# The second MLP product with seven block products in place of eight, every one of them summed over all pairs in PSUM

## The chip, the core and the metric

The kernel runs on one core of one Trainium2 chip (trn2). The metric is the time of one execution in device microseconds; it is given as the median of three runs. One further execution was profiled.

## The reference

One decoder block in float32 on a sequence of 1024 tokens with 1024 channels: three token mixers with gates, and then the MLP, the only part that the change touches:

```python
h = rmsnorm(x, g_mlp[l])
hid = jnp.square(jax.nn.relu(jnp.einsum("bsd,df->bsf", h, w_mlp_in[l])))
x = x + jnp.einsum("bsf,fd->bsd", hid, w_mlp_out[l])
...
return rmsnorm(x, g_final)
```

`w_mlp_in` (W1) is 1024 x 4096 and `w_mlp_out` (W2) is 4096 x 1024.

## The kernel before

Every float32 matrix is cut into two parts in a rounded format: ACT copies the value into `hi` (L96), and another engine takes the difference, `lo` = value - `hi` (L110 and L979). A product is then three matmuls, hi x hi, hi x lo and lo x hi (`mm3`, L151 to L153). A matmul here has 128 x 128 stationary and 128 x 512 moving elements. A tile scheduler orders every engine's instructions at build time, by priorities (`band`; band "w" goes first) and by its own model; on the chip each engine runs its list strictly in that order. SP's list is the queue of all DMAs: an issue whose buffer isn't free yet holds up every later one.

**First product** (`up_pair`, L1094 and on). The 4096 hidden columns are 16 pairs of 128-column blocks, the 1024 tokens two halves. A pair's four results, c11, c12 (first column block, token halves 1 and 2) and c21, c22, come from seven block products of 12 matmuls each instead of eight; for the first ten pairs (`EARLY`) the two that need no sums were made before, so that five are left. `load_pair` loads four 512 KB or 256 KB pieces of W1 (r0 to r3), POOL makes the four sums (L1086 to L1089), ACT and DVE cut them into hi and lo. The results sit in `hid{c}` (buffers `braw`, two). DVE clamps and squares them (L1125, L1127), and SP stores the pair to `hid_d` in DRAM, one DMA per pair.

**Second product** (`mlp_down`, L1165 and on). Eight chunks of four 128-row blocks of W2. `load_down` loads a chunk's hidden values (two loads of 1024 KB, `hr`, into `braw`) and W2 rows (four of 512 KB, `wr`); ACT makes `hhi` and `whi`, DVE `hlo`, POOL `wlo` (all 128 x 1024). For each of 8 token tiles and 2 column halves, 12 matmuls go into a PSUM bank, which DVE adds to the residual `x2` (L1181): 8 x 8 x 2 x 12 = 1536 matmuls of 512 columns (the last token tile's second half is cut in two). In the last chunk each finished token tile is normed at once: squares on ACT (L1184), a Newton root of ten small DVE operations (`rsqrt_newton`, L127 and on), the scaling of half 0 on DVE (L972) and of half 1 on ACT (L974) and POOL (L975), and the store.

The kernel has one pool, `E`, for the second product's operands; it takes the memory of the first product's (`h2T`, T2 to T4), so its first tiles wait for the first product's last matmuls.

## Time and profile before

| | us |
|---|---|
| median of 3 runs | 1498.28 (1497.91 to 1499.25) |
| the profiled execution, its own time | 1501.37 |
| its span, first to last instruction | 1499.7 |
| in it: pairs of the first product | 876 to 1132.3 |
| in it: second product, first to last matmul | 1132.3 to 1490.0 |

The span is the time between the first and the last instruction of the profiled execution; 1.67 us of that execution's time lie outside of it. In the page, a matmul's busy time overlaps with the next one's, so that TensorE's pace is read from counts in a stretch, not from the mean duration.

### The profile page before, as it was taken

How to read it: one execution, taken by the hardware profiler on the slowest of the kernel's cores; microseconds unless marked ns; L12 is line 12 of the kernel's file. 1: busy time of each engine (PE TensorE's matmuls, PEld its weight loads, DVE VectorE, ACT ScalarE, POOL GpSimd, SP SyncE). 2: the span in 40 equal slices, each digit the busy share in tenths (PEclk: the TensorE clock that was granted, in tenths of full speed). 3: DMA queues.
4: the chain of work that ended last, by engine and by line, in shares of the span. 5: the costliest groups of instructions: out<-in, count | busy, mean ns of one | idle time of the engine just before them, and what ended most of it. 6: DMA issues, size and time to landing. Idle time of an engine off the chain costs nothing.

```text
span 1499.7 us, 19772 instructions
## 1 busy us (share of the span) xinstructions
PE 1441.7 (96%) x7010; PEld 1216.6 (81%) x7010; DVE 977.4 (65%) x1911; ACT 649.2 (43%) x1271; POOL 535.1 (36%) x456
## 2 busy tenths in 40 slices
...
GB/s 218 85 58 85 102 96 39 94 42 67 51 46 61 52 47 150 140 131 199 139 223 105 164 178 140 147 161 106 113 130 230 148 63 76 112 112 113 29 14 99
DMA packets 137111, 163.61 MB, mean 109 GB/s; under 512 B 11540, under 2 KB 99636, under 8 KB 134196
## 3 DMA queue, kind: packets, MB, share of 16 engines
...
## 4 chain that ended last, share of the span: by engine, by line
PE 63%; DVE 19%; issue 6%; DMA 5%; POOL 3%; ACT 3%; SPq 0%; POOLq 0%; DVEq 0%; ACTq 0%
PE mb_dn L151 8%; PE mb_dn L152 8%; PE mb_dn L153 8%; PE mb_o L924 4%; PE gt_g L151 4%; PE gt_g L152 4%; PE gt_g L153 4%; DVE tk_jk L543 3%; DMA r<-in_w_mlp_in_dram 2%; PE mb_u L151 2%; PE mb_u L153 2%; PE mb_u L152 2%; POOL r L1087 1%; PE gt_p L152 1%; PE gt_p L151 1%
## 5 line engine op out<-in xcount | busy, mean ns | idle before, releaser
L151 PE MATMUL mb_dn<-whi,hhi 128*128 128x512 f32 (+1 forms) x516 | 199.1, 391 | 4.4 <-ACT whi L96 3.2
L153 PE MATMUL mb_dn<-whi,hlo 128*128 128x512 f32 (+1 forms) x516 | 200.7, 389 | 1.1 <-DVE hlo L979 1.1
L152 PE MATMUL mb_dn<-wlo,hhi 128*128 128x512 f32 (+1 forms) x516 | 200.9, 389 | 0.0
L1181 DVE TENSOR_TENSOR x<-x,mb_dn 128x512 f32<-128x512 f32 x129 | 87.0, 681 | 169.6 <-PE mb_dn L153 168.6
L979 POOL TENSOR_TENSOR wlo<-wr,whi 128x1024 fp32r<-128x1024 f32 x32 | 84.6, 2658 | 227.0 <-ACT whi L96 221.8
L151 PE MATMUL gt_g<-hT_hi,hi_g 128*128 128x512 f32 x384 | 153.4, 400 | 1.8 <-DVE gs L830 1.8
L153 PE MATMUL gt_g<-hT_hi,lo_g 128*128 128x512 f32 x384 | 153.5, 400 | 0.0
L152 PE MATMUL gt_g<-hT_lo,hi_g 128*128 128x512 f32 x384 | 153.4, 399 | 0.0
L151 PEld LDWEIGHTS mb_dn<-whi,hhi 128*128 128x128 f32 x516 | 97.6, 189 | 25.0 <-ACT whi L96 3.6
L153 PEld LDWEIGHTS mb_dn<-whi,hlo 128*128 128x128 f32 x516 | 97.5, 189 | 21.6 <-DVE hlo L979 1.6
L152 PEld LDWEIGHTS mb_dn<-wlo,hhi 128*128 128x128 f32 x516 | 97.4, 189 | 20.5 <-POOL wlo L979 0.5
L96 ACT ACTIVATE hi_s<-r 128x1024 fp32r<-128x1024 f32 (+1 forms) x48 | 43.6, 917 | 160.6 <-POOL r L1087 72.0
L96 ACT ACTIVATE hhi<-hr 128x1024 fp32r<-128x1024 f32 x32 | 32.7, 1049 | 182.5 <-PE mb_dn L152 159.6
L543 DVE TENSOR_SCALAR_CACHE_REDUCE tk_jk<-isc,tk_c 128x384 bf16<-128x384 f32 (+3 forms) x128 | 103.5, 809 | 2.5
L110 POOL TENSOR_TENSOR lo_g<-raw_g,hi_g 128x1024 fp32r<-128x1024 f32 x24 | 58.1, 2423 | 96.7 <-ACT hi_g L96 85.8
L979 DVE TENSOR_TENSOR lo_s<-r,hi_s 128x1024 fp32r<-128x1024 f32 (+1 forms) x48 | 51.1, 1070 | 56.8 <-ACT hi_s L96 51.1
L151 PEld LDWEIGHTS gt_g<-hT_hi,hi_g 128*128 128x128 f32 x384 | 73.6, 192 | 16.4 <-DVE gs L830 2.2
L540 ACT ACTIVATE tk_jk<-isc,tk_c 128x1024 bf16<-128x1024 f32 x64 | 73.6, 1149 | 29.7 <-DVE tk_c L552 26.9
L153 PEld LDWEIGHTS gt_g<-hT_hi,lo_g 128*128 128x128 f32 x384 | 73.5, 191 | 13.7
L152 PEld LDWEIGHTS gt_g<-hT_lo,hi_g 128*128 128x128 f32 x384 | 73.4, 191 | 13.8
L151 PE MATMUL mb_u<-T_hi,hi_s 128*128 128x512 f32 x192 | 75.6, 394 | 2.1 <-ACT hi_s L96 2.1
L1086 POOL TENSOR_TENSOR r<-r,r 128x512 f32<-128x512 f32 x16 | 21.3, 1330 | 154.9 <-DMA r<-in_w_mlp_in_dram 154.9
...
## 6 DMA issues: line engine op xcount, KB each, us to landing
...
hr<-hid_d SPq DMA_DIRECT2D x16, 1024.0 KB, 5.7
...
g_d<-gs SPq DMA_DIRECT2D x48, 256.0 KB, 2.0
gl<-g_d SPq DMA_DIRECT2D x48, 256.0 KB, 3.3
...
r<-in_w_mlp_in_dram SPq DMA_DIRECT2D x32, 256.0 KB, 3.0
...
```

Of the source, the lines that this page charges most:

```text
L96: nc.scalar.activation(o, i, AF.Copy)
L110: lo_engine.tensor_tensor(lo, raw, hi.bitcast(F32), op=ALU.subtract)
L151: nc.tensor.matmul(ps, st_hi, mv_hi, start=first, stop=False)
L152: nc.tensor.matmul(ps, st_hi, mv_lo, start=False, stop=False)
L153: nc.tensor.matmul(ps, st_lo, mv_hi, start=False, stop=last)
L540: nc.scalar.activation(jk[:, :n], isc[t], AF.Sign, bias=cand_f[:, j:j + 1], scale=-1.0, accum_out=cnt[:, j:j + 1])
L543: nc.vector.tensor_scalar(jk[:, :n], isc[t], cand_f[:, j:j + 1], 0.0, op0=ALU.is_ge, op1=ALU.add, accum_out=cnt[:, j:j + 1])
L924: nc.tensor.matmul(banks[i], st, (hi, hi, lo)[part_][:, kk_], start=(k == 0 and part_ == 0), stop=(k == KT - 1 and part_ == 2))
L979: engine.tensor_tensor(lo, raw, hi.bitcast(F32), op=ALU.subtract)
L1086: add(r2[:, lo4], r3[:, lo4], r2[:, hi4])
L1087: add(r1[:, lo4], r2[:, lo4], r0[:, lo4])
L1181: nc.vector.tensor_tensor(x2[:, t, cs], x2[:, t, cs], ps, op=ALU.add)
```

## The change

The second product becomes a seven-product scheme too. With token halves and output column halves, W2's blocks are W(i,j): column half i, row block j of a pair. In place of each pair's four hidden blocks, seven block inputs are stored, each to DRAM tensors of its own (`hid_d[0]` to `hid_d[6]`, four pairs to a tensor): c11, c21, c22, c12 - c11, c22 - (c12 - c11), c12 - c22, and c21 - c22 + c12 - c11. POOL makes the four differences (`sub`, after each pair; c12 itself isn't stored). The clamp and the square move from DVE to ACT (`square`: Relu, then Square). For the first ten pairs c11, already squared, is read back for the differences.

`down_group` then runs seven products one after the other or two together. Each has four PSUM banks (token tile i of a half), and adds all 32 row blocks into them: four steps `sc` of four pairs, 48 matmuls a step, 192 a product, 7 x 192 = 1344 in all. W2's sums (`w_s31`: two per two pairs, `w_s24`: three) are made on POOL from 512 KB blocks (`wr`, ring of 14); all `lo` parts of both operands now come from DVE. When a product is complete, `evict` adds and subtracts it into the output blocks it belongs to (`e1` to `e7`; `acc` holds a sum that several need). The groups in order: input 0; inputs 5 and 3; 4 and 2; 6; 1. Token tiles 4 to 7 are finished by `e3`, tiles 0 to 3 by `e2` after the very last product.

Two smaller edits make room and order: `up_unit`'s ring has three buffers for four, and the last pair runs its products with T3 and T4 first.

```diff
--- before.py
+++ after.py
@@ -82,7 +82,8 @@
     o_d = [dram.tile([2, P, S], F32, name=f"o_d{i}") for i in range(4)]
     g_d = [dram.tile([P, S], F32, name=f"g_d{i}") for i in range(3 * KT)]
     NPAIR = DFF // (2 * P)
-    hid_d = [dram.tile([P, 4, 512], F32, name=f"hid_d{i}") for i in range(NPAIR)]
+    hid_d = [[dram.tile([P, 4, 512], F32, name=f"hid_d{i}_{q}") for q in range(NPAIR // 4)] for i in range(7)]
     p1_d = [dram.tile([P, 512], F32, name=f"p1_d{i}") for i in range(EARLY)]
     base = ctx.enter_context(tc.tile_pool(name="base", bufs=1))
@@ -945,6 +946,8 @@
     ctxC.close()
     X3 = ctx.enter_context(tc.tile_pool(name="X3", bufs=1, reuse_waits="tile"))
     late["pool"], late["n"] = X3, 0
@@ -1048,7 +1051,7 @@
     for c in range(EARLY):
         a11, a12 = halves(load_unit(wcol[2 * c], f"wi{2 * c}", nc.vector))
         ps1, ps2 = mb_bank(f"ep{c}"), mb_bank(f"eq{c}")
-        st = M.tile([P, 2, 512], F32, tag=("stg", "u4_lo")[c % 2], name=f"st{c}")
+        st = M.tile([P, 2, 512], F32, tag="stg", name=f"st{c}", bufs=2)
         product(ps1, a11, B11)
         act_copy(st[:, 0], ps1)
         product(ps2, a12, B21)
@@ -1057,16 +1060,16 @@
         nc.scalar.activation(st[:, 1], st[:, 1], AF.Square)
         with band("w"):
             nc.sync.dma_start(p1_d[c], st[:, 0])
-            nc.sync.dma_start(hid_d[c][:, 0], st[:, 1])
+            nc.sync.dma_start(hid_d[0][c // 4][:, c % 4], st[:, 1])
     ring = {"n": 0}
     def up_unit(raw, nm, cols=slice(0, KT)):
         n = cols.stop - cols.start
         if n == KT:
-            i = ring["n"] % 4
+            i = ring["n"] % 3
             ring["n"] += 1
-            (pool, tag, bufs) = ((base, "st", 2), (base, "st", 2), (X3, "w3", 1), (M, "u4", 1))[i]
+            (pool, tag, bufs) = ((base, "st", 2), (base, "st", 2), (X3, "w3", 1))[i]
         else:
             pool, tag, bufs = M, "ud", 1
         hi, lo = (pool.tile([P, n, P], F32R, tag=f"{tag}_{part_}", name=f"{part_}_{nm}", bufs=bufs) for part_ in ("hi", "lo"))
@@ -1107,29 +1110,53 @@
         c11, c12, c21, c22 = (h[:, i] for i in range(4))
         vadd = partial(nc.vector.tensor_tensor, op=ALU.add)
+        def square(v, scale=1.0):
+            nc.scalar.activation(v, v, AF.Relu, scale=scale)
+            nc.scalar.activation(v, v, AF.Square)
+        def out_block(k, v):
+            with band("w"):
+                nc.sync.dma_start(hid_d[k][c // 4][:, c % 4], v)
+        last = c == NPAIR - 1
         m6 = times(s2, T2)
+        if last:
+            m7, m4 = times(s3, T3), times(a22, T4)
         if c >= EARLY:
             act_copy(c11, times(a11, B11))
         else:
             with band("w"):
                 nc.sync.dma_start(c11, p1_d[c])
         nc.vector.tensor_tensor(c12, m6, c11, op=ALU.subtract)
-        vadd(c22, times(s3, T3), c12)
+        vadd(c22, m7 if last else times(s3, T3), c12)
         if c >= EARLY:
             vadd(c11, times(a12, B21), c11)
-        vadd(c21, times(a22, T4), c22)
+            square(c11)
+            out_block(0, c11)
+        else:
+            with band("w"):
+                nc.sync.dma_start(c11, hid_d[0][c // 4][:, c % 4])
+        vadd(c21, m4 if last else times(a22, T4), c22)
         m5 = times(s1, T1)
         vadd(c22, m5, c22)
         vadd(c12, m5, c12)
-        for v in ([c11] if c >= EARLY else []) + [h[:, 2:4]]:
-            nc.vector.scalar_tensor_tensor(v, v, 0.0, v, op0=ALU.max, op1=ALU.mult)
+        square(h[:, 2:4])
         vadd(c12, times(s4, N22), c12)
-        nc.vector.scalar_tensor_tensor(c12, c12, 0.0, c12, op0=ALU.min, op1=ALU.mult)
-        with band("w"):
-            if c >= EARLY:
-                nc.sync.dma_start(hid_d[c], h)
-            else:
-                nc.sync.dma_start(hid_d[c][:, 1:4], h[:, 1:4])
+        square(c12, -1.0)
+        sub = partial(nc.gpsimd.tensor_tensor, op=ALU.subtract)
+        ta, tb = (M.tile([P, 2, 512], F32, tag="stg", name=f"t{nm}{c}", bufs=2) for nm in ("a", "b"))
+        out_block(1, c21)
+        out_block(2, c22)
+        sub(ta[:, 0], c12, c11)
+        out_block(3, ta[:, 0])
+        sub(ta[:, 1], c22, ta[:, 0])
+        out_block(4, ta[:, 1])
+        sub(tb[:, 0], c12, c22)
+        out_block(5, tb[:, 0])
+        sub(tb[:, 1], c21, ta[:, 1])
+        out_block(6, tb[:, 1])
     for c in range(NPAIR):
         up_pair(c)
@@ -1140,71 +1167,131 @@
     E = ctx.enter_context(tc.tile_pool(name="E", bufs=1, side="right", reuse_waits="tile"))
     gf = X3.tile([P, D], F32, tag="gvec", name="g_final_t")
+    w2 = w_mlp_out.rearrange("(c j p) d -> p c j d", j=2, p=P)
+    n_raw, n_op, n_bank = [0], [0], [0]
+    def w_block(i, j, c0):
+        n = n_raw[0]
+        n_raw[0] += 1
+        pool, tag, bufs = (X3, "xn", 2) if n < 2 else ((base, "st_raw", 1), (X3, "w3_raw", 1))[n - 2] if n < 4 else (E, "wr", 14)
+        raw = pool.tile([P, 2, 512], F32, tag=tag, name=f"wr{n}", bufs=bufs)
+        nc.sync.dma_start(raw, w2[:, c0:c0 + 2, j - 1, (i - 1) * 512:i * 512])
+        return raw
+    def add(o, a, b):
+        nc.gpsimd.tensor_tensor(o, a, b, op=ALU.add)
+        return o
+    def w_s31(c0):
+        a11, a21, a22 = w_block(1, 1, c0), w_block(2, 1, c0), w_block(2, 2, c0)
+        return add(a11, a11, a21), add(a21, a21, a22)
+    def w_s24(c0):
+        a21, a22, a11, a12 = w_block(2, 1, c0), w_block(2, 2, c0), w_block(1, 1, c0), w_block(1, 2, c0)
+        s2 = add(a11, a11, add(a21, a21, a22))
+        return s2, add(a12, a12, s2)
+    def operands(raw_t, ws):
+        ops = []
+        par = n_op[0] % 2
+        n_op[0] += 1
+        for q, w in enumerate(ws):
+            t4 = [E.tile([P, 2, 512], F32R, tag=f"{nm}{par}", name=f"{nm}{n_op[0]}_{q}", bufs=2) for nm in ("th", "tl", "sh", "sl")]
+            split(t4[2], t4[3], w, nc.vector)
+            split(t4[0], t4[1], raw_t[:, 2 * q:2 * q + 2], nc.vector)
+            ops += [tuple(v[:, u] for v in t4) for u in range(2)]
+        return ops
+    def down_group(blocks, weights, evict):
+        banks = []
+        for _ in blocks:
+            banks.append([])
+            for i in range(4):
+                n_bank[0] += 1
+                banks[-1].append((tb_bank if n_bank[0] % 4 == 0 else mb_bank)(f"dn{n_bank[0]}"))
+        for sc in range(NPAIR // 4):
+            with band("w"):
+                ws = [weights(4 * sc + 2 * q) for q in range(2)]
+            for m, k in enumerate(blocks):
+                with band("w"):
+                    raw_t = X3.tile([P, 4, 512], F32, tag="braw", name=f"tr{k}_{sc}", bufs=2)
+                    nc.sync.dma_start(raw_t, hid_d[k][sc])
+                    ops = operands(raw_t, [w[m] for w in ws])
+                for i in range(4):
+                    tsl = slice(i * P, (i + 1) * P)
+                    for u, (th, tl, sh, sl) in enumerate(ops):
+                        mm3(banks[m][i], th[:, tsl], tl[:, tsl], sh, sl, sc == 0 and u == 0, sc == NPAIR // 4 - 1 and u == 3)
+                    if sc == NPAIR // 4 - 1:
+                        evict[m](i, banks[m][i])
+    C1, C2 = H1, H2
+    acc = E.tile([P, 4, 512], F32, tag="acc", name="acc")
+    def xc(half, i, n):
+        return x2[:, 4 * half + i, (C1, C2)[n]]
+    def vacc(o, v, op=ALU.add):
+        nc.vector.tensor_tensor(o, o, v, op=op)
+    squares = {}
+    def finish_half(t, n):
+        if t not in squares:
+            squares[t] = X3.tile([P, 2], F32, tag="n_ss", name=f"ss3_{t}", bufs=8)
+        jk = X3.tile([P, 512], BF16, tag="junk", name=f"jk3_{t}{n}")
+        nc.scalar.activation(jk, x2[:, t, (C1, C2)[n]], AF.Square, accum_out=squares[t][:, n:n + 1])
+    def finish(t, pre):
+        ss = squares[t]
+        acc1 = X3.tile([P, 1], F32, tag="n_acc", name=f"acc_{t}", bufs=2)
+        nc.vector.tensor_scalar(acc1, ss[:, 1 - pre:2 - pre], 1.0 / D, EPS, op0=ALU.mult, op1=ALU.add)
+        r = rsqrt_newton(X3, ss[:, pre:pre + 1], 1, f"f_{t}", acc1)
+        for n in range(2):
+            cs = (C1, C2)[n]
+            o = x2[:, t, cs]
+            scale_half(n, o, o, r, gf[:, cs])
+            nc.sync.dma_start(out[t * P:(t + 1) * P, cs], o)
+    def e1(i, ps):
+        act_copy(acc[:, i], ps)
+        vacc(xc(0, i, 0), ps)
+        vacc(xc(1, i, 0), acc[:, i])
+    def e7(i, ps):
+        nc.vector.tensor_tensor(acc[:, i], ps, acc[:, i], op=ALU.subtract)
+    def e5(i, ps):
+        vacc(xc(1, i, 1), ps)
+        vacc(xc(1, i, 0), ps, ALU.subtract)
+    def e6(i, ps):
+        vacc(xc(1, i, 0), ps, ALU.subtract)
+        nc.vector.tensor_tensor(acc[:, i], ps, acc[:, i], op=ALU.add)
+        vacc(xc(1, i, 1), acc[:, i])
+        vacc(xc(0, i, 1), acc[:, i])
+        finish_half(4 + i, 1)
+    def e3(i, ps):
+        vacc(xc(1, i, 0), ps)
+        finish_half(4 + i, 0)
+        finish(4 + i, 0)
+    def e4(i, ps):
+        vacc(xc(0, i, 1), ps)
+        finish_half(i, 1)
+    def e2(i, ps):
+        vacc(xc(0, i, 0), ps)
+        finish_half(i, 0)
+        finish(i, 0)
     with band("w"):
         nc.sync.dma_start(gf, g_final.partition_broadcast(P))
...
-    for c in range(NC_):
-        mlp_down(c)
+    down_group([0], lambda c0: (w_block(1, 1, c0),), [e1])
+    down_group([5, 3], w_s31, [e7, e5])
+    down_group([4, 2], w_s24, [e6, e3])
+    down_group([6], lambda c0: (w_block(2, 2, c0),), [e4])
+    down_group([1], lambda c0: (w_block(1, 2, c0),), [e2])
 _INS = ["x", "mem", "positions", "g_mix", "w_in", "b_gate", "sinks", "g_mem", "w_mem_kv",
```

On POOL, in the early pairs (pair 2's differences are `ta2`, `tb2`; r1 to r3 of pair 4 are sums of W1), before:

```order
L1086 TENSOR_TENSOR r2_3_9447<-r3_3_9448,r2_3_9447 128x512
L1088 TENSOR_TENSOR r1_3_9446<-r0_3_9445,r3_3_9448 128x512
L1087 TENSOR_TENSOR r1_3_9446<-r2_3_9447,r0_3_9445 128x512
L1089 TENSOR_TENSOR r3_3_9448<-r0_3_9445,r1_3_9446 128x512
L1086 TENSOR_TENSOR r2_4_9546<-r3_4_9547,r2_4_9546 128x512
L1088 TENSOR_TENSOR r1_4_9545<-r0_4_9544,r3_4_9547 128x512
L1087 TENSOR_TENSOR r1_4_9545<-r2_4_9546,r0_4_9544 128x512
L1089 TENSOR_TENSOR r3_4_9547<-r0_4_9544,r1_4_9545 128x512
```

and with the change:

```order
L1152 TENSOR_TENSOR ta2_9487<-hid2_9409 128x512
L1156 TENSOR_TENSOR tb2_9488<-hid2_9409 128x512
L1154 TENSOR_TENSOR ta2_9487<-hid2_9409,ta2_9487 128x512
L1089 TENSOR_TENSOR r2_4_9614<-r3_4_9615,r2_4_9614 128x512
L1091 TENSOR_TENSOR r1_4_9613<-r0_4_9612,r3_4_9615 128x512
L1158 TENSOR_TENSOR tb2_9488<-hid2_9409,ta2_9487 128x512
L1090 TENSOR_TENSOR r1_4_9613<-r2_4_9614,r0_4_9612 128x512
L1092 TENSOR_TENSOR r3_4_9615<-r0_4_9612,r1_4_9613 128x512
```

Pair 4's four sums now stand between the differences of pair 2, the first of which needs pair 2's last square.

On ACT, at the end of the first product (hid15 is the last pair; `sh`, `th` are hi parts of W2 and of the stored input), before:

```order
L96 ACTIVATE hi_s4_15_10816<-r3_15_10796 128x512
L96 ACTIVATE hid15_10820<-mb_u15_2_10834 128x512
L96 ACTIVATE hhi0_10935<-hr00_10931 128x1024
L96 ACTIVATE whi0_10939<-wr0_10933 128x1024
L96 ACTIVATE hhi1_10945<-hr00_10931 128x1024
L96 ACTIVATE whi1_10949<-wr1_10943 128x1024
```

and with the change:

```order
L1115 ACTIVATE hid15_11047<-hid15_11047 128x1024
L1116 ACTIVATE hid15_11047<-hid15_11047 128x1024
L1115 ACTIVATE hid15_11047<-hid15_11047 128x512
L1116 ACTIVATE hid15_11047<-hid15_11047 128x512
L97 ACTIVATE sh1_0_11186<-wr0_11178 128x1024
L97 ACTIVATE th1_0_11184<-tr0_0_11182 128x1024
L97 ACTIVATE sh1_1_11194<-wr1_11180 128x1024
L97 ACTIVATE th1_1_11192<-tr0_0_11182 128x1024
```

The last pair's clamp and square now stand ahead of the first splits for the second product.

On SP, at the same place (`tr0_n` is input 0 of step n, 1024 KB; `wr` a W2 block, 512 KB; `hr` a hidden load), before:

```order
L1153 DMA hr00_10931<-hid_d0_85 128x2048
L1130 DMA hid_d15_100<-hid15_10820 128x2048
L1153 DMA hr01_10953<-hid_d1_86 128x2048
L1157 DMA wr2_10955<-in_w_mlp_out_dram 128x1024
L1153 DMA hr10_11199<-hid_d2_87 128x2048
L1157 DMA wr3_10965<-in_w_mlp_out_dram 128x1024
```

and with the change:

```order
L1120 DMA hid_d4_3_104<-ta15_11154 128x512
L1120 DMA hid_d6_3_112<-tb15_11155 128x512
L1218 DMA tr0_1_11252<-hid_d0_1_86 128x2048
L1178 DMA wr4_11318<-in_w_mlp_out_dram 128x2x512
L1178 DMA wr5_11320<-in_w_mlp_out_dram 128x2x512
...
L1178 DMA wr16_11630<-in_w_mlp_out_dram 128x2x512
L1218 DMA tr0_2_11322<-hid_d0_2_87 128x2048
L1178 DMA wr17_11634<-in_w_mlp_out_dram 128x2x512
L1218 DMA tr0_3_11392<-hid_d0_3_88 128x2048
```

The load for step 1 stands behind the last pair's last difference, and that for step 2 behind thirteen W2 blocks.

## Rows read from the trace of the kernel before

**Rows 1.** The page, part 1: busy us (share of the span) xinstructions.
```profile
PE 1441.7 (96%) x7010; PEld 1216.6 (81%) x7010; DVE 977.4 (65%) x1911; ACT 649.2 (43%) x1271; POOL 535.1 (36%) x456
```

**Rows 2.** Stretches: first product, transition, steady second product; us, PE, PEld, DVE, ACT, POOL, clock, DMA share, GB/s.
```profile
876.00:1132.00 256.00, 253.55 (x1107) 207.82 (x1106) 150.24 (x193) 57.62 (x67) 85.02 (x62) 0.99 0.40 133
1132.00:1156.00 24.00, 18.43 (x67) 13.76 (x66) 12.99 (x11) 8.86 (x9) 7.77 (x4) 0.86 0.71 269
1156.00:1478.00 322.00, 322.00 (x1422) 266.70 (x1422) 142.36 (x209) 61.76 (x78) 78.39 (x32) 1.00 0.24 88
```

**Rows 3.** Waits of PE from 876 to 1490: total us, times, longest.
```profile
PE mb_dn L151 <- ACT whi L96: 3.2, 1, 3.2
PE mb_u L151 <- ACT hi_s L96: 2.1, 1, 2.1
PE mb_dn L151 <- DVE hid L1126: 1.3, 1, 1.3
PE mb_dn L153 <- DVE hlo L979: 1.1, 1, 1.1
```

**Rows 4.** Stretches around the two long stalls; columns as in rows 2.
```profile
1140.00:1143.50 3.50, 3.50 (x16) 2.65 (x15) 0.00 (x0) 0.00 (x0) 0.00 (x0) 1.00 1.01 397
1143.50:1146.80 3.30, 0.12 (x2) 0.01 (x1) 1.92 (x2) 2.95 (x3) 0.00 (x0) 0.83 0.98 408
1146.80:1152.00 5.20, 5.20 (x12) 3.79 (x13) 3.31 (x3) 2.95 (x3) 3.89 (x2) 0.50 0.75 263
...
944.60:947.00 2.40, 0.33 (x3) 0.06 (x1) 0.75 (x3) 1.06 (x1) 2.32 (x2) 1.00 0.09 34
947.00:952.00 5.00, 5.00 (x14) 3.57 (x15) 5.00 (x7) 0.63 (x1) 0.15 (x1) 0.66 0.54 156
```

**Rows 5.** The splits of the second product by tile: ns min/median/max.
```profile
L979 DVE TENSOR_TENSOR hlo<-hr,hhi x32: 1210/1226/2823, 1135.5 to 1409.5; 128x1024 fp32r<-128x1024 f32 x32
L979 POOL TENSOR_TENSOR wlo<-wr,whi x32: 2388/2412/3386, 1128.4 to 1413.3; 128x1024 fp32r<-128x1024 f32 x32
```

**Rows 6.** Timeline of POOL and DVE in the second product: start, us.
```profile
1184.08 1.23 DVE L979 TENSOR_TENSOR hlo<-hr,hhi 128x1024 fp32r<-128x1024 f32 x1 [0.86 <-ACT hhi L96]
1185.08 5.85 POOL L979 TENSOR_TENSOR wlo<-wr,whi 128x1024 fp32r<-128x1024 f32 x2 [13.34 <-ACT whi L96]
...
1185.98 2.69 DVE L979 TENSOR_TENSOR hlo<-hr,hhi 128x1024 fp32r<-128x1024 f32 x1
```

**Rows 7.** Groups on ACT: count | busy, mean ns | idle before.
```profile
L96 ACT ACTIVATE whi<-wr 128x1024 fp32r<-128x1024 f32 x32 | 33.6, 1051 | 47.6 <-DMA wr<-in_w_mlp_out_dram 47.1 <-PE mb_dn L153 0.5
L1056 ACT ACTIVATE st<-st 128x512 f32<-128x512 f32 x10 | 6.3, 629 | 6.7 <-DVE st L1055 6.7
```

**Rows 8.** Groups on POOL and DVE; columns as in rows 7.
```profile
L1086 POOL TENSOR_TENSOR r<-r,r 128x512 f32<-128x512 f32 x15 | 19.4, 1293 | 147.1 <-DMA r<-in_w_mlp_in_dram 147.1
L979 DVE TENSOR_TENSOR lo_s<-r,hi_s 128x1024 fp32r<-128x1024 f32 x18 | 22.4, 1263 | 37.2 <-ACT hi_s L96 31.5 <-DMA hid_d<-st 5.7
L1126 DVE TENSOR_TENSOR hid<-mb_u,hid 128x512 f32<-128x512 f32 x8 | 5.4, 678 | 0.0
L972 DVE SCALAR_TENSOR_TENSOR x<-x,y_f,g_final_t 128x512 f32<-128x512 f32 x6 | 4.5, 743 | 0.0
```

**Rows 9.** DMA issues: KB each, median us from issue to landing.
```profile
hr<-hid_d SPq DMA_DIRECT2D x16, 1024.0 KB, 5.7
r<-in_w_mlp_in_dram SPq DMA_DIRECT2D x32, 256.0 KB, 3.0
```

**Rows 10.** Timeline of the tail.
```profile
1489.72 0.28 PE L153 MATMUL mb_dn<-whi,hlo 128*128 128x256 f32 x1
...
1493.38 0.16 DVE L136 SCALAR_TENSOR_TENSOR v_f<-ss,acc 128x1 f32<-128x1 f32 x1 [0.64 <-ACT jk L1184]
...
1495.17 0.16 DVE L147 SCALAR_TENSOR_TENSOR y_f<-t_f,y_f 128x1 f32<-128x1 f32 x1
1495.42 0.72 ACT L1203 ACTIVATE x<-x,y_f 128x512 f32<-128x512 f32 x1 [2.07 <-DVE y_f L147]
```

58 lines of the change are left out of this document (removed).

## Prediction

> **What bounds the kernel now.** I read the page first: PE is busy for 96% of the span [rows 1], so the kernel gains where matmuls go away and loses where PE starts to wait. The table of stretches [rows 2] then gives PE's pace in the part that the change replaces: 1422 matmuls in 322 us without a gap and at a granted clock of 1.00, that is 0.2264 us each. In that stretch DVE is busy 44%, ACT 19%, POOL 24% and the DMA engines 24%: the second product waits for nothing but PE. The list of PE's waits [rows 3] shows how little is lost elsewhere: four waits of over 1 us in 600 us. Two of them cost more than themselves [rows 4]: after the idle 3.17 us before 1146.8, and after the 2.07 us before 947, the clock stands at its lower level (0.50, i.e. 1.2 GHz) for a while. From 1146.8 to 1152 PE began 12 matmuls in 5.2 us where 23 fit, a loss of 11 x 0.2264 = 2.5 us. After the waits of 1.27 and 1.13 us around 1135 the pace stayed.
>
> **1. Matmuls taken away.** 1536 become 1344, all of 512 columns. 192 x 0.2264 [rows 2] = **-43.5 us**, on the path, since PE is the path there. The order holds 192 matmuls for each of seven products, so this part is certain; the rest is what is given back.
>
> **2. The shared work of POOL and DVE.** Before, DVE split the hidden values (32 operations) and POOL the weights (32). Now DVE makes all 112 `lo` parts and POOL 40 sums, all 128 x 1024 from SBUF to SBUF. Alone, such a POOL operation takes 2.41 us and a DVE one 1.23 [rows 5]. Together they exclude each other: two POOL operations from 1185.08 took 5.85 us, which is 2 x 2.41 plus about one DVE operation, and the DVE operation begun at 1185.98 inside the first took 2.69 [rows 6]. I price them as taking turns. The Trainium skill says the same (SBUF — State Buffer, section "SBUF: two separate sides"): a DVE operation with two SBUF inputs and a GpSimd operation hold a shared port pair for the whole instruction, and the other blocks; rows 6 agree, and by this rule the term is the one that follows, while without it the term would be nothing.
>
> A step of four pairs costs PE 48 x 0.2264 = 10.87 us per product, 21.7 for two. Inputs 5 and 3 need 4 sums and 8 splits per step: 4 x 2.41 + 8 x 1.23 = 19.5 us of turns. Inputs 4 and 2 need 6 and 8: **24.3 us in 21.7**. POOL may run ahead, but SP's order couples the two: each hidden load stands behind W2 blocks whose buffers come free only by sums of the step ahead. So count from the landing of the first W2 blocks that are summed (behind part 3's load at 11 us and 1024 + 6 x 512 KB, 4.2 MB at 397 GB/s [rows 4], so some 24 us after the first product's end) to the load of input 4 for step 2: 39 sums (94.0) and 54 splits (66.4) with some 3 us of other adds make 163 us, so that load goes out at 187 us. With 5.7 us to land [rows 9] and the first splits, its matmuls start at about 196. PE would be there at 16 (lost by part 3) + 192 x 0.2264 + 12 x 10.87 = 190. That is 6 us late if the two never leave the turn unused, 14 with 5% unused: I take **+10**. Bounds: 0, if the two overlap after all; 27, if in each of the eight blocks of inputs 4 and 2 four sums and four splits strictly alternate behind the first ACT split (4 x 3.64 + 1.05 = 15.6 us, less the 1.36 us of matmuls that need only the first half, against 10.87).
>
> **3. The transition.** Before: from 1132.3 to 1490.0 are 357.7 us for 1536 x 0.2264 = 347.7 us of work, so 10.0 us are lost, nearly all ahead of 1156 [rows 2]. Now, from the last matmul of the first product (t = 0): DVE adds the last block (0.68 [rows 8]), ACT clamps and squares it (2 x 0.63 [rows 7]), and only then come the first splits, in ACT's order: the first matmul has both hi parts at 2 + 2 x 1.05 [rows 7] = 4.05. Such a stall is followed by the low clock, 2.5 more. Step 0 ends at 4.05 + 2.5 + 10.87 = 17.4. Meanwhile POOL makes the last pair's four differences (1.29 each [rows 8]) in turns with three DVE splits, till 10.8; SP waits for the last of them, so step 1's hidden load goes out at 11 and lands at 16.7 (5.7 [rows 9]), its splits at 17.8 and, on DVE, 21.2: 0.4 and some 1.8 us of waiting. Step 1 ends at 30.5. Step 2's load stands behind thirteen W2 blocks: 1024 + 13 x 512 + 1024 KB = 8.9 MB, at the 397 GB/s of a full stretch [rows 4] 22.5 us from 11, so 33.5, and its split and the semaphores bring 35.5: a stall of 5 us and 2.5 of low clock. Sum: 4.05 + 2.5 + 2.2 + 5 + 2.5 = 16.3 against 10.0: **+6**. Bounds: +1 (only the first stall as worked out, the loads in time) and +11 (DMA at the 263 GB/s of the mixed stretch [rows 4], which brings step 2's data 11 us later, half of it hidden by the stalls ahead).
>
> **4. The first product.** The clamp and square go from DVE to ACT, which has room (58 us busy of 256 [rows 2]); 0 on the path but for the latency. POOL gets four differences beside four sums. For an early pair PE needs 60 x 0.2264 = 13.6 us; POOL and DVE's turns are 8 x 1.29 + 2 x 1.26 + 0.68 = 13.5 [rows 8], nearly as much. The chain, from the end of a pair: last add and square 3.0 us (ACT has the next split in between), three differences, the sums of the pair after next with a fourth difference between them and one DVE split: the sum that the main operand needs is done at 3.0 + 7 x 1.29 + 1.26 = 13.3, its split at 14.4. Most pairs now begin with another product (2.7 us), so the operand is wanted at 16.3; those that begin with it (about every third) wait 0.8. The W1 piece for these sums is issued after the split that frees its buffer and lands 3.0 us later [rows 9], at about 6, before POOL comes to it. That a wait here is close, the 2.07 us at 947 show. Six late pairs have 19 us each and hide it all. I take **+3**; bounds 0 and +10 (one us for each early pair). The stores and reads of 256 KB more than double SP's issues per pair, but the DMA engines are at 40% there [rows 2].
>
> **5. The tail.** Before: last matmul's end 1490.0, end of the span 1499.7, so 9.7. After: the four last token tiles are complete 2.72 us apart, but each asks of DVE 0.68 for the add, 1.95 for the root (from 1493.38 to 1495.33 [rows 10]) and 0.74 [rows 8]: 3.4 us, so the fourth's root ends some 6.1 us after the last matmul. Then 0.72 on ACT [rows 10], 1.3 on POOL (it multiplied ahead before), and 3.6 from there to the end as before (1496.14 to 1499.7): 11.7. **+2.5** with turns lost between POOL and DVE; bounds +1 and +4.
>
> **Sum:** -43.5 + 10 + 6 + 3 + 2.5 = **-22 us**, from a span of 1499.7 to 1477.7. The profiled execution's own time, 1501.37, is 3.1 us above the median of 1498.28; against the median the forecast is **1476 us**. All ends at their best give -41.5, all at their worst +8.5.
>
> **Rivals.**
> - *All of it is hidden* (+2 to +8 given back): POOL runs far enough ahead that the turns never come late. For it: 19.5 of 21.7 us in the first pair of inputs leave room to run ahead, and W2's ring has 14 buffers. Against it: SP's order. Time: 1498.3 - 37 to 41 = 1457 to 1462. Chance 0.20.
> - *The first product is starved*: if ACT's order or SP's queue adds 1.5 us to the chain of part 4 in each early pair, and some of these waits reach 2.07 us and draw 1.8 us of low clock (14 matmuls in 5 us for 22 [rows 4]), it gives back 16 us more: 1492. For it: 13.5 of 13.6 us. Chance 0.10.
> - *Slower than before*: the turns in the second product make PE wait at the start of most blocks by 2 us or more, and each wait brings the low clock. One such block costs 2.07 + 1.8 = 3.9 us [rows 4]. Of the 16 blocks of the four summed inputs, 12 would cost 47 us in place of the 10 of part 2: 1476 + 37 = 1513. It decides from 8 blocks on (31 us). For it: strict turns give 3.3 us of waiting per block. Against it: POOL has only 3 sums per block on average, not 4, and the waits are spread. Chance 0.12.
> - That the change wouldn't take the matmuls away is excluded by the order.
>
> **How the numbers follow.** The forecast (faster, 1464 to 1488) has 0.58, the rivals 0.20, 0.10 and 0.12. A measurement of this kernel tells 0.2% (3 us) from no change. Slower by more than that is the third rival and a little of the second: 0.10; within 0.2% (1495.3 to 1501.3): 0.05, from the edges of both; faster: 0.85. The range of 8 in 10 takes in the lower edge of the first rival and the second: 1459 to 1496.
>
> **What would show it.** Right: about 1344 matmuls on the second product's banks at 0.2264 us; a wait of some 4 us at its start and one at step 2, ended by a split of a hidden load; POOL's L1182 and DVE's L982 with means well over 2.41 and 1.23 in the groups of inputs 5, 3, 4 and 2, and PE waits there of about 10 us in sum; a tail near 12 us. Wrong: waits of PE on early pairs of over 10 us in sum, a clock well under 1.00 between the second and the fifth product, or no waits there at all.

## The result, and the profile after

The changed kernel takes **1479.8 us** (median of 4 runs, 1476.49 to 1481.63) against 1498.19 for the kernel before on the same chip: ratio **0.9873, 95% interval 0.9854 to 0.9893**. The forecast was 1476 (1459 to 1496), faster. The profiled execution took 1476.49, its span is 1474.4 (before: 1499.7). The page's part 1, which answers to [rows 1]: 204 matmuls fewer on PE (12 of them because the last half tile is no longer cut in two).

```profile
PE 1397.2 (95%) x6806; PEld 1174.0 (80%) x6806; DVE 1041.8 (71%) x1871; ACT 753.4 (51%) x1397; POOL 659.4 (45%) x526
```

The table of stretches answers to [rows 2] (us; PE, PEld, DVE, ACT, POOL busy and counts; granted clock; DMA share; GB/s). Before, only PE was full behind 1156. Now the DMA engines are full in 1150 to 1170, POOL in 1170 to 1200, and DVE in 1250 to 1300; from 1350 on PE is alone again.

```profile
876.00:1130.00 254.00, 246.64 (x1082) 202.03 (x1081) 125.90 (x151) 103.37 (x130) 160.53 (x120) 1.00 0.60 191
...
1134.00:1150.00 16.00, 12.00 (x43) 9.66 (x43) 10.96 (x7) 7.26 (x9) 7.87 (x4) 0.79 0.53 175
1150.00:1170.00 20.00, 13.11 (x56) 9.89 (x54) 9.45 (x7) 6.03 (x6) 10.47 (x4) 0.93 1.04 393
1170.00:1200.00 30.00, 26.94 (x107) 21.82 (x107) 27.73 (x10) 14.21 (x16) 29.60 (x11) 0.88 0.82 310
...
1250.00:1300.00 50.00, 49.38 (x215) 39.62 (x214) 50.00 (x29) 18.61 (x20) 38.95 (x14) 1.00 0.71 252
...
1350.00:1460.00 110.00, 110.00 (x487) 91.07 (x486) 71.97 (x125) 47.90 (x69) 6.36 (x4) 1.00 0.33 116
```

PE's waits from 876 to 1475 answer to [rows 3] (total us, times, longest). The two long ones, 4.00 and 8.05 us, wait for the split of a hidden load (`th`); five in the first product, 7.4 us together, wait for the split of W1's sums (`hi_s`).

```profile
PE mb_dn L152 <- ACT th L97: 12.6, 3, 8.1
PE mb_u L152 <- ACT hi_s L97: 7.4, 5, 2.7
PE mb_dn L153 <- DVE sl L982: 2.2, 4, 0.9
PE mb_dn L154 <- DVE tl L982: 1.7, 2, 1.2
```

The timeline gives the marks between which the stages are measured (start, us): the first product's first matmul on `h2T` and its last matmul, the two long stalls, the last matmul of the first group, the last matmul of all, and two steps of the tail [rows 10].

```profile
880.70 0.39 PE L152 MATMUL mb_u<-h2T_hi,hi_s 128*128 128x512 f32 x1
...
1133.62 0.39 PE L154 MATMUL mb_u<-h2T_hi,lo_s 128*128 128x512 f32 x1
1138.00 1.65 PE L152 MATMUL mb_dn<-sh,th 128*128 128x512 f32 x3 [4.00 <-ACT th L97]
...
1172.28 0.80 PE L152 MATMUL mb_dn<-sh,th 128*128 128x512 f32 x1 [8.05 <-ACT th L97]
...
1196.34 0.39 PE L154 MATMUL tb_dn<-sh,tl 128*128 128x512 f32 x1
...
1462.96 0.39 PE L154 MATMUL tb_dn<-sh,tl 128*128 128x512 f32 x1
...
1469.13 0.16 DVE L148 SCALAR_TENSOR_TENSOR y_f<-t_f,y_f 128x1 f32<-128x1 f32 x1
...
1470.12 1.26 POOL L978 TENSOR_TENSOR x<-x,g_final_t 128x512 f32<-128x512 f32 x1 [1.94 <-ACT x L977]
```

The first two of these marks before:

```profile
882.90 0.39 PE L151 MATMUL mb_u<-h2T_hi,hi_s 128*128 128x512 f32 x1
...
1132.11 0.39 PE L153 MATMUL mb_u<-h2T_hi,lo_s 128*128 128x512 f32 x1
```

By these marks the 25.3 us between the two spans come from: the second product, 1132.5 to 1490.0 = 357.5 us before and 1134.0 to 1463.35 = 329.35 now, -28.15 (that is the -43.5 of the matmuls, and **15.3 given back**); the first product, 249.6 before and 253.3 now, **+3.7**; the tail, 9.7 and 11.05, **+1.35**; and 2.2 us by which this execution reached 880.70 earlier. Those 2.2 us were there at the first early block product already (816.2 for 818.4), ahead of all code that changed. The two profiled executions lie at the two ends of their kernels' spread: the one before took 3.2 us more than its median, the one now 3.3 us less. That is why the spans differ by 25.3 us and the medians by 18.4.

The groups of instructions from 1126 to 1340 show POOL's sums and DVE's splits (count | busy, mean ns | idle before). Alone they take 2.41 and 1.23 us [rows 5, 6].

```profile
L1182 POOL TENSOR_TENSOR wr<-wr,wr 128x1024 f32<-128x1024 f32 x40 | 123.5, 3094 | 43.7 <-DMA wr<-in_w_mlp_out_dram 42.4
L982 DVE TENSOR_TENSOR tl<-tr,th 128x1024 fp32r<-128x1024 f32 x36 | 82.4, 2300 | 25.0 <-ACT th L97 25.0
L982 DVE TENSOR_TENSOR sl<-wr,sh 128x1024 fp32r<-128x1024 f32 x36 | 71.6, 1997 | 12.2 <-ACT sh L97 12.1
```

SP's queue behind the first product: the last pair's last store, step 1's load, thirteen W2 blocks in 13.22 us, step 2's load, and, after one more block and step 3's load, seven more blocks. Step 2's load was asked for at 1159.27 and split from 1171.2 on.

```profile
1144.16 0.32 SPq L1120 DMA_DIRECT2D hid_d<-tb  x1
1144.66 0.32 SPq L1218 DMA_DIRECT2D tr<-hid_d  x1
1145.03 13.22 SPq L1178 DMA_DIRECT2D wr<-in_w_mlp_out_dram  x13
1159.27 0.58 SPq L1218 DMA_DIRECT2D tr<-hid_d  x1
...
1163.32 14.01 SPq L1178 DMA_DIRECT2D wr<-in_w_mlp_out_dram  x7
```

Over the whole run, a 1024 KB hidden load takes 7.1 us to land for 5.7, and W1's `r` 3.9 for 3.0 [rows 9].

```profile
tr<-hid_d SPq DMA_DIRECT2D x28, 1024.0 KB, 7.1
...
r<-in_w_mlp_in_dram SPq DMA_DIRECT2D x32, 256.0 KB, 3.9
```

### The profile page after: what moved, and what is told of

Same layout as the page of the kernel before. It is cut to its first block, busy times and chain, and to the rows that moved or that the text cites. A ratio compares the mean times of both kernels' runs of the same rounds, so it can differ in the third digit from the quotient of the medians.

```text
span 1474.4 us, 19857 instructions
## 1 busy us (share of the span) xinstructions
PE 1397.2 (95%) x6806; PEld 1174.0 (80%) x6806; DVE 1041.8 (71%) x1871; ACT 753.4 (51%) x1397; POOL 659.4 (45%) x526
## 5 line engine op out<-in xcount | busy, mean ns | idle before, releaser
L982 DVE TENSOR_TENSOR tl<-tr,th 128x1024 fp32r<-128x1024 f32 x56 | 107.7, 1930 | 57.0 <-ACT th L97 55.1
L152 PE MATMUL mb_dn<-sh,th 128*128 128x512 f32 x336 | 132.6, 396 | 12.6 <-ACT th L97 12.6
L1182 POOL TENSOR_TENSOR wr<-wr,wr 128x1024 f32<-128x1024 f32 x40 | 123.5, 3094 | 43.7 <-DMA wr<-in_w_mlp_out_dram 42.4
L153 PE MATMUL mb_dn<-sl,th 128*128 128x512 f32 x336 | 132.9, 397 | 2.2 <-DVE sl L982 2.2
L154 PE MATMUL mb_dn<-sh,tl 128*128 128x512 f32 x336 | 130.7, 393 | 1.7 <-DVE tl L982 1.7
L97 ACT ACTIVATE th<-tr 128x1024 fp32r<-128x1024 f32 x56 | 58.5, 1051 | 137.7 <-PE tb_dn L153 114.2
L982 DVE TENSOR_TENSOR sl<-wr,sh 128x1024 fp32r<-128x1024 f32 x56 | 96.8, 1733 | 12.4 <-ACT sh L97 12.3
L152 PEld LDWEIGHTS mb_dn<-sh,th 128*128 128x128 f32 x336 | 64.2, 191 | 27.4 <-ACT th L97 13.9
L153 PEld LDWEIGHTS mb_dn<-sl,th 128*128 128x128 f32 x336 | 64.2, 191 | 17.7 <-DVE sl L982 4.6
L154 PEld LDWEIGHTS mb_dn<-sh,tl 128*128 128x128 f32 x336 | 63.8, 190 | 15.9 <-DVE tl L982 2.6
## 6 DMA issues: line engine op xcount, KB each, us to landing
g_d<-gs SPq DMA_DIRECT2D x48, 256.0 KB, 2.0
gl<-g_d SPq DMA_DIRECT2D x48, 256.0 KB, 3.4
hid_d<-hid SPq DMA_DIRECT2D x38, 256.0 KB, 3.5
r<-in_w_mlp_in_dram SPq DMA_DIRECT2D x32, 256.0 KB, 3.9
```

Source lines behind the costliest of these rows:

```text
L97: nc.scalar.activation(o, i, AF.Copy)
L152: nc.tensor.matmul(ps, st_hi, mv_hi, start=first, stop=False)
L153: nc.tensor.matmul(ps, st_hi, mv_lo, start=False, stop=False)
L154: nc.tensor.matmul(ps, st_lo, mv_hi, start=False, stop=last)
L982: engine.tensor_tensor(lo, raw, hi.bitcast(F32), op=ALU.subtract)
L1182: nc.gpsimd.tensor_tensor(o, a, b, op=ALU.add)
```

## The experiments

Twelve kernels, numbered in the order in which they ran; "first product", "second product", "first group" (its part up to the last matmul of input 0) and "behind it" are measured between the marks above in the one profiled execution; "ratio" is to the kernel before, on the same chip. PE needs 10.88 us for a step without a wait, so 43.5 for the first group and 261.1 behind it. The expectations count the first group to the copy of its last bank, which begins 1.0 to 4.2 us later (1199.0 in the changed kernel, so 65.0 and 264.4 us there).

| | ratio, interval | first product | second product | of it first group | behind it |
|---|---|---|---|---|---|
| changed kernel | 0.9873 [0.9854, 0.9893] | 253.3 | 329.4 | 62.7 | 266.6 |
| 1 load into `acc` | 0.9900 [0.9884, 0.9915] | 256.2 | 334.2 | 58.5 | 275.7 |
| 2 sums on DVE | 0.9854 [0.9832, 0.9876] | 255.3 | 326.7 | 62.4 | 264.2 |
| 3 no sums | 0.9848 [0.9832, 0.9864] | 256.3 | 323.7 | 62.5 | 261.1 |
| 4 differences on DVE | 0.9843 [0.9824, 0.9863] | 253.9 | 324.7 | 58.8 | 265.9 |
| 5 = 1 + 2 + 4 | 0.9750 [0.9737, 0.9762] | 256.0 | 314.0 | 50.6 | 263.4 |
| 6 ring buffers | 0.9895 [0.9882, 0.9908] | 255.2 | 334.9 | 55.6 | 279.4 |
| 7 second `r3` buffer | 0.9818 [0.9805, 0.9831] | 244.5 | 331.2 | 62.9 | 268.3 |
| 8 squares on DVE | 0.9924 [0.9909, 0.9938] | 259.7 | 333.4 | 64.3 | 269.2 |
| 9 = 5 + 7 | 0.9699 [0.9681, 0.9716] | 244.1 | 315.3 | 50.5 | 264.8 |
| 10 = 9 + 6 | **0.9646** [0.9630, 0.9662] | 244.1 | **307.2** | 46.1 | 261.1 |
| 11 = 6 + 2 | 0.9767 [0.9750, 0.9783] | 256.7 | 314.6 | 53.5 | 261.1 |
| 12 changed kernel again | 0.9871 [0.9854, 0.9888] | 254.0 | 330.1 | 62.8 | 267.2 |

**1. Step 2's load no longer behind W2.**

```diff
-raw_t = X3.tile([P, 4, 512], F32, tag="braw", name=f"tr{k}_{sc}", bufs=2)
+raw_t = acc if (k, sc) == (0, 2) else X3.tile([P, 4, 512], F32, tag="braw", name=f"tr{k}_{sc}", bufs=2)
```

> Edit: the first group's hidden load for step 2 goes into the tile `acc`, which nothing uses yet, so that its issue no longer stands behind thirteen loads of W2. Queue theory (the 8.05 us stall at step 2 comes from SP's order alone: the load waits for a buffer, and behind the W2 loads): the load goes out some 13 us earlier, the stall at step 2 and the low clock behind it (0.63 in 1170 to 1180) vanish, 8 to 10 us of the 21.4 lost before the first group's end come back, ratio to the changed kernel about 0.994 (1468 to 1471 us). Rival, bandwidth (the DMA engines are full at 390 GB/s, so what one load gains another loses): a stall of similar size appears at step 3 or with inputs 5 and 3, and less than 3 us come back.

The stall at step 2 was gone, so SP's order was its cause. But the kernel was no faster: the second product took 334.2 us, 5 more. PE's waits from 1139 on are now waits for DVE's splits (`sl`, `tl`: 11.3 us for 3.9):

```profile
PE mb_dn L153 <- DVE sl L982: 8.1, 6, 3.1
PE mb_dn L152 <- ACT th L97: 4.6, 2, 4.0
PE mb_dn L154 <- DVE tl L982: 3.2, 3, 2.1
```

In the two stretches where these waits lie, DVE is busy for 33.00 of 33 and 54.74 of 55 us (in the changed kernel 32.66 and 53.09, and PE 31.80 and 53.76), and the clock falls to 0.88 on the mean of the first:

```profile
1182.00:1215.00 33.00, 26.95 (x101) 20.53 (x101) 33.00 (x17) 13.97 (x16) 27.94 (x10) 0.88 0.67 244
1255.00:1310.00 55.00, 51.12 (x223) 41.05 (x221) 54.74 (x32) 19.52 (x20) 43.51 (x16) 1.00 0.73 253
```

The rival's effect, but not yet its cause: late blocks or turns? The next two runs and the fifth tell.

**2 and 3. The sums on DVE, and left out.** In `add`, `nc.gpsimd` becomes `nc.vector`; in run 3 the line goes.

> Edit: the forty sums of W2 go from POOL to DVE, so that POOL has nothing to do in the second product. Turn theory (POOL and DVE exclude each other, L1182 takes 3.1 us for 2.41 and DVE's split 1.8 to 1.9 for 1.23): with one engine doing all of it a step of inputs 4 and 2 costs 14 x 1.23 = 17 us of 21.7, splits take 1.23 again, and the waits after the first group's end (3.4 us) go to about 1; in the transition, sums no longer delay the splits. Gain 2 to 4 us. Rival, order on DVE (sums now stand ahead of splits in one list, and DVE's list also has the evictions): splits come late, the stretch after the first group loses more than 3.4 us; 0 to 8 us slower.

> Edit: the forty sums of W2 are left out, so the products of inputs 5, 3, 4 and 2 take operands that were never summed; nothing else changes. It bounds what the sums cost in any way. Turn theory as predicted (10 us from inputs 5, 3, 4 and 2): about 10 us faster there alone. Theory after the reading of the trace (the sums run ahead of PE and cost 3.4 us at most after the first group): 3 us or less there; in the transition W2's buffers come free without waiting for POOL, so that SP's queue moves earlier, but the hidden load for step 2 still stands behind thirteen W2 loads: the 8 us stall stays within 2 us.

Run 3 gives the price of the sums in the changed kernel: 329.4 - 323.7 = 5.7 us, and the first group is as long as before (62.5 for 62.7), so the transition owes them nothing. Behind it run 3 takes 261.1 us, 24 steps of 10.88: without the sums PE waits for nothing there. Run 2 wins about half of that: a sum on DVE takes 1.22 us, half of POOL's price alone, and the splits are back at 1.26 to 1.28.

```profile
L1182 DVE TENSOR_TENSOR wr<-wr,wr 128x1024 f32<-128x1024 f32 x40 | 48.8, 1223 | 24.9 <-DMA wr<-in_w_mlp_out_dram 24.4
L982 DVE TENSOR_TENSOR tl<-tr,th 128x1024 fp32r<-128x1024 f32 x36 | 45.9, 1282 | 21.8 <-ACT th L97 21.7
L982 DVE TENSOR_TENSOR sl<-wr,sh 128x1024 fp32r<-128x1024 f32 x36 | 45.0, 1258 | 6.7 <-ACT sh L97 6.7
```

So DVE does the sums and the splits together in 139.7 us, where the splits alone cost it 154.0 us beside POOL's sums (82.4 + 71.6). The Trainium skill warns of this in "Perfetto Trace Analysis" (section "Optimizing Scalar/DVE Operations"): since GpSimd and DVE share an SBUF port, offloading between the two might not help. The trace agrees, 139.7 us against 154.0. By the ratios alone the two runs can't be told from the changed kernel (the intervals overlap); the stages can.

**4. The differences on DVE.** `sub = partial(nc.vector.tensor_tensor, op=ALU.subtract)` for `nc.gpsimd`.

> Edit: the four differences of a pair go from POOL to DVE. Turn theory for the first product (the four sums and four differences on POOL, 8 x 1.29 us in turns with DVE, make the early pairs late; 7.4 us of waits there against 2 or 3 before): POOL's chain gets 5.2 us shorter, DVE's 2.7 us longer, the waits of over 1 us on early pairs vanish, 2 to 4 us faster before 1134; and the last pair's differences are done some 4 us earlier, so step 1's load too, up to 2 us more. Rival (DVE's list is the one that is late: adds of a pair stand behind the differences, which wait for ACT's squares): waits move to the DVE splits and adds, 0 to 8 us slower.

Wrong for the first product: the waits stay (7.6 us for 7.4), so POOL's turns with the differences are not their cause. Right for the transition: the last store went out at 1138.85 for 1144.16, step 2's stall fell to 5.6 us and the first group to 58.8. The group of POOL's first sum shows what POOL is idle for now, mostly W1's load (128.8 of 150.5 us; that such waits are what makes PE late, run 7 has to show):

```profile
L1089 POOL TENSOR_TENSOR r<-r,r 128x512 f32<-128x512 f32 x15 | 20.1, 1341 | 150.5 <-DMA r<-in_w_mlp_in_dram 128.8 <-DVE tb L1158 13.0 <-DMA hid_d<-ta 8.6
```

**5. The first, second and fourth edits together.**

> Edit: the load for step 2 into `acc` (as in the first experiment), and both the forty sums and the pairs' differences on DVE (as in the second and the fourth). The first experiment took the stall at step 2 away, and lost 9 us more after the first group. Lead theory (POOL got its W2 blocks later, and its sums at 2.4 us and more had no reserve to catch up): with the sums on DVE at 1.23 us, the stretch after the first group's end goes back to some 262 us (it was 262.0 with the sums on DVE alone, 273.4 in the first experiment), the first group takes 57 to 61 us, sum about 10 us faster than the changed kernel, ratio to before 0.978 to 0.982. Rival, bandwidth (the W2 blocks themselves land too late whichever engine adds them): 8 us or more of the loss after the first group stay, ratio 0.984 or more.

1463.57 us, a ratio of 0.9750 to the changed kernel's 0.9873: some 18 us won, more than the 10 expected, where the first edit alone won nothing. The second product takes 314.0 us, and behind its start no wait is longer than 0.9:

```profile
PE mb_dn L152 <- ACT th L97: 4.0, 1, 4.0
PE mb_dn L153 <- DVE sl L982: 2.4, 4, 0.9
```

The bandwidth rival falls: the same bytes now land in time for a second product that is 20 us shorter than in run 1.

**6. The first splits ahead of the last squares.**

```diff
-t4 = [E.tile([P, 2, 512], F32R, tag=f"{nm}{par}", name=f"{nm}{n_op[0]}_{q}", bufs=2) for nm in ("th", "tl", "sh", "sl")]
+if n_op[0] == 1 and q == 0:
+    t4 = [v.rearrange("p (u k) c -> p u (k c)", u=2) for v in ring_pair("s") + ring_pair("t")]
+    t4 = t4[2:] + t4[:2]
+else:
+    t4 = [E.tile([P, 2, 512], F32R, tag=f"{nm}{par}", name=f"{nm}{n_op[0]}_{q}", bufs=2) for nm in ("th", "tl", "sh", "sl")]
```

`ring_pair` returns the next hi and lo buffers of the ring that `up_unit` uses.

> Edit: the operands of the second product's first half step lie in buffers of the first product's weights that come free some 20 us before its end, in place of memory that is free only behind its last matmul; in ACT's list these two splits now stand ahead of the last pair's squares. Memory theory (the 4.0 us stall at the second product's start is ACT's squares and splits behind the last matmul): it falls below 1 us. SP's order moves too: step 2's load stands behind eight W2 blocks, no longer thirteen, so the 8 us stall should fall by 5 x 1.33 us of DMA time less the 4 us that PE arrives earlier, to some 5 us. First group 65 to some 57 to 60 us. Rival (what is gained comes back as waits in inputs 5, 3, 4 and 2, as in the first experiment): the stretch behind it goes from 264 to 268 us or more, and less than 3 us are won in all.

The first stall is gone, but my place for the next one was wrong: it is step 1 now that waits 7.2 us, since its load is still behind the last pair's stores (issued at 1149.33, 10 us behind the last matmul).

```profile
PE mb_dn L154 <- DVE tl L982: 7.7, 4, 2.9
PE mb_dn L152 <- ACT th L97: 7.5, 2, 7.2
PE mb_dn L153 <- DVE sl L982: 3.7, 3, 2.8
```

Behind the first group it takes 279.4 us, 12.8 more than the changed kernel, with waits for DVE as in run 1. The rival was right: what is gained comes back there, and the kernel is no faster than the changed one (0.9895 to 0.9873). Experiment 11 tells what that was.

**7. A second buffer for `r3`.**

```diff
-r3 = X3.tile([P, KT, P], F32, tag="gvec", name=f"r3_{c}")
+r3 = (X3, M)[c % 2].tile([P, KT, P], F32, tag=("gvec", "r3b")[c % 2], name=f"r3_{c}")
```

> Edit: every second pair's block `r3` of W1 gets a buffer of its own, so that its load no longer waits for the split of the pair before. Load theory for the 7.4 us of waits in the first product (with the differences on DVE they stayed, and POOL waited for W1's loads there: SP can issue them only after the split that frees `r3`, and that split stands behind ACT's squares): waits of over 0.5 us on `hi_s` fall to 2 us in sum, first product 253.5 to 248 to 250 us, ratio 0.981 to 0.984. Rival, POOL's turns (sums and differences on POOL take 8 x 1.29 us and more per pair): waits stay above 5 us.

As the load theory said, and more: no wait of PE is left from 876 to 1132, and the first product takes 244.5 us, less than before the change (249.6). Same sums, same differences on POOL: what made the pairs late was the load of `r3`, which waited for the split that frees its only buffer.

**8. The squares back on DVE.** `scalar_tensor_tensor(v, v, 0.0, v, op0=max or min, op1=mult)` in `square`.

> Edit: the clamp and square of the pairs go back to DVE, one operation for ACT's two. If ACT's squares delay the split that frees `r3` (they stand ahead of it by 2.1 us), the waits in the first product shrink from 7.4 to about 4 us, and the stall at the second product's start shrinks from 4.0 to some 2.5 us, since ACT's first splits no longer stand behind the last squares: 3 to 6 us faster than the changed kernel, ratio 0.983 to 0.986. Rival: DVE is the one that is late with turns (1.3 us more work per pair there, in turns with POOL's eight operations): waits of 7 us or more stay, no gain.

The guess for the first product failed and its rival held: the waits for `hi_s` stay (8.0 us), waits of 2.6 us for DVE's split `lo_s` are added, and the first product takes 259.7 us. The first stall shrinks as guessed, to two waits of 1.74 and 1.03 us for DVE's splits, but nothing is won by it: step 2 waits 9.35 us, for its load lands when it lands. The kernel is slower than the changed one (0.9924 to 0.9873, intervals apart), so giving ACT the squares was right.

**9. Four edits together.**

> Edit: four edits together: step 2's load into `acc`, sums on DVE, differences on DVE, and a second buffer for `r3`. If the losses lie in separate stages (transition and second product: 16 us won together in the fifth experiment; first product: some 7 us in the seventh), they add: 1455 to 1458 us, ratio 0.969 to 0.972. Rival (the differences on DVE delay the splits that the earlier W1 loads now wait for, or the earlier end only meets the same W2 loads): less than 3 us better than the fifth, ratio 0.973 or more.

1454.6 us: the gains of the first product and of the second add up.

**10 and 11. The ring buffers where the sums are on DVE.**

> Edit: the four edits and the ring buffers of the sixth experiment. If the sixth gave its gain back only to POOL's sums, the 4.0 us stall and the low clock behind it are now won for good: 3 to 6 us better than the four alone, ratio 0.966 to 0.969. Rival (the load for step 1 stands behind the stores of the last pair and lands at a fixed time, so the stall moves to step 1): within 2 us of the four alone.

> Edit: the ring buffers of the sixth experiment, and the sums on DVE; differences stay on POOL. The sixth took 278 us behind the first group against 264 in the changed kernel. If POOL's sums in turns with DVE's splits set that, it goes back to 262 to 266, the first group stays near 57, ratio 0.976 to 0.981. Rival (late W2 blocks: the DMA engines are as full): 272 us or more behind the first group, ratio 0.985 or more.

**1446.82 us** (1444.34 to 1447.92), 33 us under the changed kernel on the same chip (run 12). The ring buffers, with which the second product grew by 5.5 us in run 6, win 8 here, more than expected; PE waits 2.0 us in the whole second product, and DVE, with all sums and splits, is busy for 89% at most:

```profile
1126.60:1180.00 53.40, 51.44 (x226) 41.88 (x225) 41.67 (x42) 26.13 (x30) 0.00 (x0) 1.00 0.98 366
1180.00:1230.00 50.00, 50.00 (x222) 41.40 (x221) 42.49 (x38) 19.67 (x20) 0.00 (x0) 1.00 0.92 333
1230.00:1280.00 50.00, 50.00 (x222) 41.41 (x221) 44.44 (x45) 15.64 (x16) 0.00 (x0) 1.00 0.87 303
```

Run 11 has one edit more than run 6, the sums on DVE: 334.9 falls to 314.6, and the 279.4 us behind the first group to 261.1, where nothing is lost. Its only waits in the second product are those for the load:

```profile
PE mb_dn L152 <- ACT th L97: 7.7, 2, 6.5
```

So the 18.3 us lost there in run 6 came from POOL's sums beside DVE's splits, not from late blocks.

**12. The changed kernel again.**

> The changed kernel itself once more, unedited, so that it stands on the same chip beside the others: ratio 0.985 to 0.990. If the spread of its runs (1476.5 to 1481.6) comes from whether the clock drops at the first product's waits, runs with a mean clock of 0.983 are 3 us or more longer than those with 0.99, and the profile of this one shows a different clock in 940 to 1040 with the same waits.

1480.34 us. Its stages repeat within 0.8 us. The runs with a mean clock of 0.990 and 0.984 took 1477.94 and 1482.25; the two between them took 1480.3. The clock from 940 to 1040 is 0.98 in this profile and 1.00 in the first, as guessed. Two profiles are not the whole spread, though: runs 1, 2, 3, 6 and 11, whose edits leave the first product alone, took 255.2 to 256.7 us there, so a difference of 3 us in that stage says nothing by itself.

## Why the prediction was right, and where it was not

The sign and the size of the sum hold: 22 us forecast, 18.4 measured between the medians. In part that is luck. By the stages of the two profiled executions the turns and the tail cost less than forecast (by 4.5 and 1.15 us), the transition and the first product more (by 3.4 and 0.7), and these errors offset each other. The terms one by one:

1. **Matmuls, -43.5:** held. Where PE is alone it begins 487 matmuls in 110 us, 0.2259 each, against 0.2264 assumed.

2. **Turns of POOL and DVE, +10:** that the two exclude each other holds, as the 3.1 and 2.0 to 2.3 us of sums and splits and run 2 show. The term was too large: the changed kernel loses 5.5 us behind the first group (266.6 for 24 steps of 10.88, and 261.1 in run 3 without the sums). The step that failed is the meeting point. The load of input 4 for step 2 was to go out at t = 187, and its matmuls to begin at 196, 6 us after PE could (t counts from the first product's end). It went out at 1306.98 (t = 173), and PE, busy with the steps before, came to its matmuls at t = 199: it was not late at all. I had priced a turn by the durations of one sum and one split, 3.64 us. Where the two alternate, DVE's splits begin 3.35 us apart (1227.45, 1230.80, 1234.15, 1237.48), and 1.14 apart where POOL is idle (1204.30, 1205.44, 1206.57), so that a sum takes 2.21 of the turns. From POOL's first sum at 1159.4 to that load, 39 sums and 50 splits (54 in the forecast) at these prices are 143 us of the 147.6 that passed, in place of 163. What was lost instead is lost in single steps, in six of the first ten behind the first group (1.54, 1.23, 0.28, 0.29, 0.58 and 1.58 us), at waits for DVE's splits of 3.4 us in sum; "about 10 us" of such waits was my sign of being right.

   The forecast held PE's lateness from the transition against the turns once, at that load; the runs show that it counts in every step. Take a stall away and leave the turns (runs 1 and 6), and 14.6 and 18.3 us are lost behind the first group; take the turns away alone (run 3), and only 5.7 us are won in the second product. Stall and turns together are worth 15.4 in run 5, which also has the differences on DVE, worth 4.7 there by themselves (run 4).

3. **Transition, +6:** too small, inside its bounds: the first group loses 19.2 us (62.7 for 43.5) where 16.3 were forecast, against 9.8 before, **+9.4**. The first stall is 4.00 us (4.05 forecast), and step 1's load went out at 1144.66 (t = 10.7; forecast 11). The step that failed is the landing of step 2's load: I took the bytes ahead of it by 397 GB/s and had it at 33.5. It was split from 1171.2 (t = 37.2). From 1144.66 to 1171.2 the DMA engines moved 9.8 MB, at 371 GB/s, for the 8.9 MB that I counted: they were full (393 GB/s in 1150 to 1170), but what was issued behind that load had part of them. From its own issue to its split it took 11.9 us. So the stall was 8.05 us for 5; the low clock behind it cost what was forecast (45 matmuls in 1170 to 1185, where PE's 12.7 us would have held 56: 2.5 us).

4. **First product, +3:** 3.7 and 4.4 in the two profiles of the changed kernel, 5.6 to 7.1 in the five runs named under 12: too small on the whole, inside its bounds. The reason was not right. I priced POOL's turns; run 4 took the differences off POOL to no effect, and run 7, which leaves them there, removed every wait. The chain went through the W1 piece that I had landing "before POOL comes to it": its load stands behind the split that frees `r3`, and from issue to landing it takes 3.9 us, not 3.0.

5. **Tail, +2.5:** 1.35. The last scaling ran 1469.32 to 1471.38 on ACT and POOL, and from there 3.0 us to the end, where I had taken 3.6.

**The rivals.** "All of it is hidden" failed by more than the turns: without their 5.5 us some 15 are given back, where it had 8 at most. "The first product is starved" needed 16 us more and got one in the profile, 3 to 4 in the five runs named under 12. "Slower" needed eight late blocks in the second product; the changed kernel has one wait over 1 us there. Runs 1 and 6 show that this rival was nearer than it looked: each has three waits of 2 to 3 us for DVE, and a mean clock of 0.80 to 0.89 in the 15 us at or behind each.

**Still open:** of the 18.3 us that run 6 loses behind its first group, 9.9 are waits for DVE's splits; how much of the rest is the clock behind them was not separated. Run 7 shows that `r3`'s buffer made the pairs late, but not which part of the change did that, since with the same single buffer PE waited only 2.1 us before [rows 3]: the squares on ACT, the ring of three buffers for four, or SP's longer list. Run 8 doesn't settle it, since DVE was late there. And a faster transition with the sums on POOL, but issued earlier, wasn't tried.
